# Row sums by ScalarE's queue in attention, an own tile for attention's output copy, DFT tables loaded in layer 0's last chunk, and z as the fourth chunk

## The chip, the core and the metric

The kernel runs on one core of a Trainium2 chip. The metric is the device time of one execution in microseconds (us); the time of a kernel is the median of its runs. The engines are named as in the profile: PE (TensorE matmuls) with PEld (its weight loads), DVE (VectorE), ACT (ScalarE), POOL (GpSimd) and SP (SyncE). SP only issues DMAs here; "SPq", "ACTq" and "POOLq" are DMA issues and waits in an engine's instruction queue.

## What is computed

A trunk of two layers over 2048 tokens of 1024 channels, in float32. Cut to what matters:

```python
# layer 0: norm, one projection, short gated convolution beside a Fourier mixer, output projection
a_x, a_b, a_c, a_z, b_u, b_z = split(rms_norm(x) @ w_in)          # 6 x 512 columns
y_a = a_b * conv3(a_c * a_x) * silu(a_z)
y_b = fft2(u by groups of 128 channels, axes=(tokens, channels)).real * silu(b_z)
x = x + concat([y_a, y_b]) @ w_out
# layer 1: norm, q/k/v/z projection, rotary, 8 query heads over 2 kv heads, softmax over all 2048 keys
o = softmax(q k^T / sqrt(128)) v
x = x + (o * silu(z)) @ w_out
out = rms_norm(x)
```

## The kernel before, in words

Every matrix is split into two fp32r parts, a high part (a cast, by ACT) and a low part (source minus high part, by DVE or POOL; `split`, lines 40 to 44), and every product is three matmuls (`mm3`, lines 56 to 60). The split of a large tile is therefore one ACT and one DVE (or POOL) instruction at lines 42 and 44. In the input projection of layer 0 a product of two 2 x 2 block matrices is done with seven block products instead of eight (`product`, lines 387 to 419): the operand blocks and their sums are called 11, s2, s3, s1, 12, 22, s4, and PE takes them in that order. After each block product a hook may run (`follow`), which is how other work is placed in the program beside a chunk.

**Layer 0's input projection** (`layer0_in`) goes through eleven chunks, i = 0 to 10. A conv chunk computes 128 channels of the convolution branch and ends in taps on ACT and DVE (lines 602 to 606) and products on POOL (lines 626 and 638); a simple chunk is u (copied out) or z (SiLU, line 659). Chunks 0 to 4 work on tokens 0 to 1023: the conv chunks 1, 2, 3, 4 and then z. Chunks 5 to 10 work on tokens 1024 to 2047: u, four conv chunks, z. The operands of the second half are made meanwhile by `operands` (lines 227 to 252), called four times through `prepare(k)` from hooks: each call takes three places of a small ring of tiles ("ring_o"), loads x, normalises it on DVE (line 433), forms sums and differences on POOL (line 240) and saves seven blocks to DRAM. After chunk 4 `load_operand` brings them back and splits them (line 44 once per half block).

**The Fourier mixer** (`fourier`) takes four groups g. `fold(c, g)` loads u of a group and folds it by its symmetries on DVE and POOL (lines 717 to 740, tile "uo"); `fold_transposes` turns the result on PE (tile "fqt"); then four products with DFT tables (tiles "fme" and "fm", PSUM "pfz"), a second, short transform (`second`), and a product with silu(z) (`finish`). Folds 0 and 1 run in hooks of chunk 10. The tables are loaded by GpSimd's queue at the head of `fourier` (lines 766 to 774). Operands, folds, tables and rings all come from one pool of nine large tiles, tag "S"; a tile can be taken when the last reader of the one before is done.

**Attention** (`Attention`) has 32 groups of one block of 128 queries and one kv head, with four heads each. Its order is written out by hand in lists of steps (`SLOT`, `DRAIN`): one slot per head and group, S score matmuls, M/C/N maximum, E exponent with row sums, T transposes of the probabilities (PE), H and L their split (ACT line 1356, DVE line 1360), O the product with v. PE, DVE, ACT and SP keep this order. Once per group G adds up the row sums and takes the reciprocal (line 1382), D writes them to DRAM (line 1389, tile "l" to "ld"), B reads them back as a broadcast (line 1398, tile "lb") together with z (line 1401, tile "az") and multiplies both on POOL (line 1403). When the last O of a group is done, `finish` copies the PSUM tile on ACT into the broadcast's own tile "lb" (line 1408) and POOL multiplies again (line 1409). There is one PSUM tile for O.

**The end of attention.** `DRAIN` is the slot list of the last groups. In it `layer1_out_start` issues the loads of the first operands ("a_o") and weights ("ring_r" from "wo") of the output projection, and ten steps W split them, one at a time, with the low parts on POOL. After attention `layer1_out` splits the rest, and PE starts the output projection (PSUM "po").

Outside attention only PE's order is fixed by hand; DVE, ACT, POOL and SP are ordered when the program is built, by a simulated timeline and priorities.

Of the kernel before, what the change touches and what calls it, by code (L numbers as in the profile page):

```python
# [15 lines left out]
F32 = mybir.dt.float32  # L16
F32R = mybir.dt.float32r
AF = mybir.ActivationFunctionType
ALU = mybir.AluOpType
# [4 lines left out]
P = 128  # L24
S = 2048
# [14 lines left out]
def split(nc, src, hi, lo, hi_eng="act", lo_eng="dve"):  # L40

    first = nc.vector.tensor_copy(hi, src) if hi_eng == "dve" else nc.scalar.copy(hi, src)  # L42
    eng = nc.vector if lo_eng == "dve" else nc.gpsimd
    return first.ins, eng.tensor_tensor(lo, src, hi, op=ALU.subtract).ins  # L44
# [377 lines left out]
def layer0_in(c):  # L422
# [64 lines left out]
    def mean(tb):  # L487
        d = None
        if tb < 2:
            d = c.RD0[tb] = c.dram.tile([4, P], F32, name=f"rd_n0_{tb}", tag=f"rd_n0_{tb}")  # L490
        bc[tb] = rstd_pe(c, [accs[:, tb * TB:(tb + 1) * TB] if tb < 2 else acc1[0][:, tb - 2]], f"n0_{tb}", TB, d)

    def bcast(tb):
        RB[tb] = c.evp.tile([P, TB], F32, tag="ev", name=f"rb_n0_{tb}")[:]
        nc.scalar.copy(RB[tb], bc[tb]())
# [157 lines left out]
    def simple_chunk(pr, W, dst, silu, name, hooks={}):  # L653
# [9 lines left out]

        st.product(W, out, f"p{name}_", hooks)

    def next_weights(i):
        return st.all_weights(c.w0[(i + 2) % 6 if i < 5 else i - 4], f"w{i + 1}")

    def norm1(x, j, k):
        norm(x, RB[2 + j], k)  # L670
# [1 line left out]
    def prepare(k):  # L672
        return lambda: st.operands(k, [c.x_T[2], c.x_T[3]], norm1)

    hooks = {0: first_hooks,
             2: {"s2": lambda: mean(2), "s1": lambda: (bcast(2), mean(3)),
                 "22": lambda: (bcast(3), st.held.clear()), "s4": prepare(0)},
             3: {"s2": prepare(1), "s1": prepare(2), "22": prepare(3)}, 10: c.fourier_first}
    for i in range(11):
        pr, ch = divmod(i, 5) if i < 5 else (1, i - 6)  # L680
        W = W0
        if 0 < i < 10:
            W0 = next_weights(i)
        if 0 <= ch < 4:
            conv_chunk(pr, ch, W, hooks.get(i, {}))
        elif ch == 4:
            simple_chunk(pr, W, c.bz, True, f"z{pr}", hooks.get(i, {}))
        else:
            simple_chunk(pr, W, c.uT, False, "u1")
        if i == 0:  # L690
            all_k("s4", d2)
            st.A.pop("21")
            w1("21", "t4", "22")
            start.__exit__(None, None, None)
            W0 = W1[0]
            stats1()
        if i == 4:
            for j, op in enumerate(A_OPS):
                st.load_operand(op, c.aT[j], "1")
            c.alt = c.evp.tile([P, TB], F32, name="alt", tag="ev")  # L700
            c.dm = c.evp.tile([P, 2, 2, P], F32R, name="dm", tag="ev")
            h = TB // 2
            nc.gpsimd.memset(c.alt[:, 0:h:2], 1.0)
            nc.gpsimd.memset(c.alt[:, 1:h:2], -1.0)
            nc.gpsimd.memset(c.alt[:, h:TB], 0.0)
            nc.gpsimd.dma_start(c.dm[:], c.dmat)
        if i == 9:
            nc.sync.dma_start(c.yT[1, 0:4, :, TB - 1].rearrange("c p -> p c"), yedge[:])
# [43 lines left out]
        split(nc, pt[:], qt[:, 0, j], qt[:, 1, j])  # L752


def fourier(c):


# [5 lines left out]
    zs, qa, dcos, nyqs = mix[:, 0:TB], mix[:, TB:TB + h], mix[:, TB + h:TB + h + P], mix[:, D - 16:D]  # L763
    xss = st.etile("fxs")
    fb = c.big.tile([P, 2, S], F32, tag="S", name="fb0")
    even = c.big.tile([P, 2, 2, 2, 2, h], F32R, tag="S", name="fme")
    for j in range(2):
        nc.gpsimd.dma_start(even[:, j], c.feven[j])
    M = []
    for j in range(2):  # L770
        m = c.big.tile([P, 2, 4, TB], F32R, tag="S", name=f"fm{j}")
        for i in range(2):
            nc.gpsimd.dma_start(m[:, i], c.fmat[j, i])
        M.append(m)
    nc.sync.dma_start(dcos, c.dcos_d)
    QT = c.QT
    NY = [None] * 4
# [438 lines left out]
class Attention:  # L1216
# [167 lines left out]
    def D(self, k):  # L1384
        if k % NTT:
            return
        st = self.st[k // NTT]
        st.d = self.c.dram.tile([4, P], F32, name=f"ld{st.name}", tag=f"ld{st.name}")
        self.nc.sync.dma_start(st.d[:].rearrange("h t -> t h"), st.l[:])

    def B(self, k):

        if k % NTT != 8:
            return
        st = self.st[k // NTT]
        c, nc, nm, d = self.c, self.nc, st.name, st.d
        st.rb = self.zp.tile([P, TB], F32, tag="rb", name=f"lb{nm}")
        nc.sync.dma_start(st.rb[:], d[:].rearrange("h t -> (h t)").partition_broadcast(P))
        qt, kvh = st.g
        st.zt = self.zp.tile([P, TB], F32, tag="z", name=f"az{nm}")  # L1400
        nc.sync.dma_start(st.zt[:].rearrange("p (h t) -> p h t", h=4),
                          c.zT[kvh * 4:kvh * 4 + 4].rearrange("h p t -> p h t")[:, :, qt * P:(qt + 1) * P])
        nc.gpsimd.tensor_tensor(st.zt[:], st.zt[:], st.rb[:], op=ALU.mult)  # L1403

    def finish(self, st):
        c, nc = self.c, self.nc
        qt, kvh = st.g
        c.last_copy = nc.scalar.copy(st.rb[:], st.po[:]).ins  # L1408
        nc.gpsimd.tensor_tensor(st.zt[:], st.zt[:], st.rb[:], op=ALU.mult)  # L1409
        self.ended.append(lambda: nc.sync.dma_start(  # L1410
            c.oT[qt // 4, kvh * 4:kvh * 4 + 4].rearrange("h p t -> p h t")[:, :, (qt % 4) * P:(qt % 4 + 1) * P],
            st.zt[:].rearrange("p (h t) -> p h t", h=4)))


def layer1_out_start(c, lp):

    nc = c.tc.nc
    st = c.pairs
    st.renew()
    c.W11 = tuple(lp.tile([P, 4, TB // 2], F32R, tag="w0", name=f"wo1_0_11{n}") for n in "hl")  # L1420
    st.A["11"] = st.atile("a11_o0")
    src = [c.oT[0], c.oT[1]]
    for k in (slice(0, 2), slice(2, 4)):
        st.fetch(st.raw("11", k), src, "11", k)
    c.wo1_raw = st.raw_weights(c.wo1[0])
    st.A["12"] = st.atile("a12_o0")
    for k in (slice(0, 2), slice(2, 4)):
        st.fetch(st.raw("12", k), src, "12", k)

    def w11(sl):  # L1430
        split(nc, c.wo1_raw["11"][:, sl], c.W11[0][:, sl], c.W11[1][:, sl], lo_eng="pool")

    return ([lambda k=k: st.split("11", k, "pool") for k in range(4)] + [lambda j=j: w11(slice(j, j + 2)) for j in (0, 2)]
            + [lambda k=k: st.split("12", k, "pool") for k in range(4)])


def layer1_out(c, lp):
# [128 lines left out]
def trunk_kernel(ctx, tc, x_T, g0, w0, cw, wo0, g1, w1, qg, kg, wo1, gf, cosT, sinT, fmat, feven, dmat, dcos, out_T, scratch=None):  # L1566
# [41 lines left out]
    with ExitStack() as es_w:  # L1608
        with ExitStack() as es_ps:
            c.ps = es_ps.enter_context(tc.tile_pool(name="ps", bufs=8, space=PSUM))  # L1610
            c.big = ctx.enter_context(tc.tile_pool(name="big", bufs=9))
            c.evp = ctx.enter_context(tc.tile_pool(name="ev", bufs=2))
            c.wp = es_w.enter_context(tc.tile_pool(name="w", bufs=8, side="right", reuse_waits="tile"))
            with ExitStack() as es_e:
                c.ep = es_e.enter_context(tc.tile_pool(name="e", bufs=4, side="right", reuse_waits="tile"))
                c.pairs = Pairs(c)
                c.QT = [None] * 4

                def fold0():
                    c.rb01 = c.pairs.gtile("rb01")[:, 0:D]  # L1620
                    for tb in range(2):
                        bcast_d(c, c.RD0[tb], f"u_{tb}", tile=c.rb01[:, tb * TB:(tb + 1) * TB])
                    c.fold0 = fold(c, 0)

                def fold1():
                    c.fold1 = fold(c, 1)

                c.fourier_first = {"s2": fold0, "12": fold1, "22": lambda: fold_transposes(c, 0, c.fold0[0])}
                layer0_in(c)
                c.pairs.renew()  # L1630
                fourier(c)
                layer0_out(c)
                layer1_in(c)
        c.fp = es_w.enter_context(tc.tile_pool(name="zf", bufs=3, side="right", reuse_waits="tile"))
        load_kv(c)
        es_q = ctx.enter_context(ExitStack())
        qp = es_q.enter_context(tc.tile_pool(name="attq", bufs=2, reuse_waits="tile"))
        es_a = ctx.enter_context(ExitStack())
        pools = [es_a.enter_context(tc.tile_pool(name=n, bufs=b, space=PSUM, reuse_waits="tile"))
                 for n, b in (("pss", 4), ("pst", 3), ("pso", 1))]  # L1640
        fill = c.filler(pools[1])
        for _ in range(7):
            next(fill)
        att = Attention(c, qp, *pools, groups, fill, [6, 6, 6, 5, 2])
        for n in range(5):
            att.slot(n, att.FIRST)
            if n == 1:
                c.silu_z(att.exp.ins)
# [113 lines left out]
```

## Time and profile before

| | |
|---|---|
| median of 3 runs | 2339.57 us (2337.32 to 2339.77) |
| the profiled execution's own time | 2335.91 us |
| its span, first to last instruction | 2334.1 us |
| busy: PE / DVE / ACT / POOL | 2265.6 / 1531.9 / 1201.3 / 571.1 us |
| mean granted TensorE clock | 0.990 |
| moved by DMA | 413.99 MB, mean 177 GB/s |

A row of the timeline has the start, the duration, the engine, the line, the operation, "out<-in" by tile names, the shapes and a count of merged instructions; in brackets stands the idle time of the engine just before it and what ended that. A row of the list of waits has who waited for whom, the total, the number of times and the longest. A row of the stretches has each engine's busy time in that stretch, PE's granted clock, the mean busy share of the 16 DMA engines and their rate. The four groups of work stand in the span at about these places: layer 0's input projection up to 514 us, the Fourier mixer to 586, the output projection of layer 0 and the projections of layer 1 to 1200, attention to 2125, the output projection of layer 1 to the end.

### The profile page before, as it was taken

Reading aid. Unit: us, or ns where it says so; the run is one execution under the profiler, and the core shown is the slowest. Engines: PE = TensorE matmul, PEld = TensorE weight load, DVE = VectorE, ACT = ScalarE, POOL = GpSimd, SP = SyncE. Lnnn points to the kernel's source line nnn. Section 1 sums busy time; section 2 is a strip of 40 time slices with the busy share of each in tenths; the row PEclk is TensorE's granted clock in tenths of the full one; section 3 lists DMA queues with packets and bytes.
Section 4 is the critical chain, followed back from the end, with each engine's and each line's share of the span. In section 5 each row is a group of like instructions: output and inputs, shape, how many; then the busy total and the mean of one; then the engine's idle time right before and its main releaser. Section 6 shows DMA issues by size and latency. Waiting matters only on the chain. (4 is left out here: it accounts for less than half of the span.)

```text
span 2334.1 us, 34356 instructions
## 1 busy us (share of the span) xinstructions
PE 2265.6 (97%) x12450; PEld 1917.2 (82%) x12450; DVE 1531.9 (66%) x2469; ACT 1201.3 (51%) x2638; POOL 571.1 (24%) x418
## 2 busy tenths in 40 slices
PE   9989899988999999999999999999999999997998
PEld 7877688877888899889987888888888888886887
DVE  7967867679642445425548888788788788775235
ACT  5442432224332345424547777777777777775212
POOL 2566535444232132103201100010001000003212
PEclk9999999999999999999999999999999999998999
DMA  4244742247756534533566767676666676668553
GB/s 164 86 149 155 253 138 73 63 171 268 266 187 201 145 119 134 163 102 127 171 235 185 205 203 202 196 200 204 193 200 197 193 195 198 201 187 269 180 189 127
DMA packets 260281, 413.99 MB, mean 177 GB/s; under 512 B 37136, under 2 KB 157072, under 8 KB 258320
## 3 DMA queue, kind: packets, MB, share of 16 engines
q1 hardware_dynamic: 257840, 404.17, 55.0%
q0 software_dynamic: 1008, 6.55, 0.8%
q8 instruction: 99, 1.62, 0.3%
q10 hardware_dynamic: 1264, 1.07, 0.1%
q14 instruction: 70, 0.57, 0.1%
HBM read 190.92 MB, written 86.59 MB: 119 GB/s over the span
## 5 line engine op out<-in xcount | busy, mean ns | idle before, releaser
L1314 DVE TENSOR_REDUCE mx<-s 128x1 f32<-128x512 f32 x512 | 351.0, 687 | 172.6 <-PE s L60 170.9
L1333 ACT ACTIVATE praw<-s,nb,qs 128x512 f32<-128x512 f32 x512 | 401.3, 800 | 18.2 <-DVE nb L1323 12.1
L1356 ACT CAST pr<-t 128x512 fp32r<-128x512 f32 x512 | 290.8, 600 | 181.7 <-PE t L1344 181.7
L1360 DVE TENSOR_TENSOR pr<-t,pr 128x512 fp32r<-128x512 f32 x512 | 329.3, 680 | 13.2 <-ACT pr L1356 11.4
L1344 PEld LDWEIGHTS t<-ident_r,P 128*128 128x128 f32 x2048 | 202.0, 140 | 36.9 <-DVE pr L1360 1.1
L58 PE MATMUL o<-pr,kv 128*128 128x512 f32 x512 | 212.2, 414 | 2.5 <-ACT pr L1356 2.1
L58 PE MATMUL s<-kv,aq 128*128 128x512 f32 x512 | 211.0, 412 | 2.4 <-DMA aq<-qT 1.2
L1344 PE MATMUL t<-ident_r,P 128*128 128x128 f32 x2048 | 203.8, 243 | 0.9 <-DVE pr L1360 0.9
L60 PE MATMUL o<-pr,kv 128*128 128x512 f32 x512 | 202.5, 395 | 0.0
L59 PE MATMUL o<-pr,kv 128*128 128x512 f32 x512 | 202.2, 395 | 0.2 <-DVE pr L1360 0.2
L60 PE MATMUL s<-kv,aq 128*128 128x512 f32 x512 | 201.9, 394 | 0.0
L59 PE MATMUL s<-kv,aq 128*128 128x512 f32 x512 | 200.8, 392 | 0.0
L1403 POOL TENSOR_TENSOR az<-az,lb 128x512 f32<-128x512 f32 x32 | 41.4, 1295 | 477.6 <-DMA az<-zT 454.8
L958 POOL TENSOR_TENSOR acc<-acc,sq 128x512 f32<-128x512 f32 x48 | 69.0, 1438 | 228.4 <-ACT sq L956 210.5
L60 PEld LDWEIGHTS o<-pr,kv 128*128 128x128 f32 x512 | 96.2, 188 | 23.2
L60 PEld LDWEIGHTS s<-kv,aq 128*128 128x128 f32 x512 | 96.1, 188 | 22.5
L58 PEld LDWEIGHTS s<-kv,aq 128*128 128x128 f32 x512 | 95.8, 187 | 21.3 <-ACT praw L1333 3.2
L1333 ACT ACTIVATION_READ_ACCUMULATOR praw<-s,nb,qs 128x1 f32 x512 | 112.7, 220 | 0.0
L58 PEld LDWEIGHTS o<-pr,kv 128*128 128x128 f32 x512 | 96.0, 187 | 19.7 <-ACT pr L1356 2.5
L59 PEld LDWEIGHTS o<-pr,kv 128*128 128x128 f32 x512 | 96.5, 188 | 17.7 <-DVE pr L1360 0.5
L59 PEld LDWEIGHTS s<-kv,aq 128*128 128x128 f32 x512 | 96.3, 188 | 17.2
L1409 POOL TENSOR_TENSOR az<-az,lb 128x512 f32<-128x512 f32 x32 | 42.0, 1311 | 253.0 <-ACT lb L1408 250.1
(644 smaller groups left out, 5836.8 us busy)
## 6 DMA issues: line engine op xcount, KB each, us to landing
P<-praw SPq DMA_DIRECT2D x256, 512.0 KB
ring_r<-w SPq DMA_DIRECT2D x80, 512.0 KB
ring_o<-x_T SPq DMA_DIRECT2D x32, 512.0 KB
ring_r<-wo SPq DMA_DIRECT2D x32, 512.0 KB
qT<-ring_o SPq DMA_DIRECT2D x64, 256.0 KB
aq<-qT SPq DMA_DIRECT2D x31, 512.0 KB
x1T<-po_t SPq DMA_DIRECT2D x16, 512.0 KB
a_x<-x1T SPq DMA_DIRECT2D x16, 512.0 KB
```

What stands on the lines that cost most here:

```text
L58: nc.tensor.matmul(ps, lh, rh, start=first, stop=False, skip_group_check=shared)
L59: nc.tensor.matmul(ps, lh, rl, start=False, stop=False, skip_group_check=shared)
L60: nc.tensor.matmul(ps, ll, rh, start=False, stop=last, skip_group_check=shared)
L958: nc.gpsimd.tensor_tensor(a, a, sq, op=ALU.add)
L1314: self.nc.vector.tensor_reduce(st.mx[h][:, b:b + 1], st.banks[h, b][:], op=ALU.max, axis=AX.X)
L1333: self.exp = nc.scalar.activation(raw[:, b % 2], st.banks.pop((h, b))[:], AF.Exp, bias=st.nb[h][:], scale=self.c.qs[:, st.g[0], st.g[1], h ...
L1344: self.nc.tensor.transpose(pt[:, h * P:(h + 1) * P].bitcast(F32R), st.Ps[h // 2][:, h % 2, kt // 8, (kt % 8) * P:(kt % 8 + 1) * P], self.c ...
L1356: self.nc.scalar.copy(pr[:, 0], pt[:])
L1360: self.nc.vector.tensor_tensor(pr[:, 1], pt[:], pr[:, 0], op=ALU.subtract)
L1403: nc.gpsimd.tensor_tensor(st.zt[:], st.zt[:], st.rb[:], op=ALU.mult)
L1409: nc.gpsimd.tensor_tensor(st.zt[:], st.zt[:], st.rb[:], op=ALU.mult)
```

## The change

1. **Order of the chunks.** A list gives the order: 1, 2, 3, 5, 4 for the first half of the tokens, so that z comes fourth and the last conv chunk fifth; the second half is as before. The four calls of `prepare` move into the z chunk, behind its products 11, s3, 12 and s4.
2. **DFT tables.** Their loads, still by GpSimd's queue, move into hooks of chunk 10: the even table behind product s3, the two odd ones behind s1 and 12. `fold(c, 1)` moves out of that chunk to a place just ahead of `fourier`.
3. **Row sums.** D writes the 128 x 4 reciprocals as 128 rows of four, by ScalarE's queue, instead of transposed as four rows of 128 by SyncE's queue. B reads the broadcast in that order, and POOL's first product takes it through a strided view. The load of z moves from B to D, two slots earlier.
4. **Copy of attention's PSUM.** `finish` copies into a tile of its own ("oc", one buffer) instead of into "lb".
5. **Splits at the end of attention.** Of the ten W steps the low parts are made by DVE instead of POOL, and the weights' two steps come behind the first two steps of operand 11 instead of behind all four.

```diff
+    chunks = (1, 2, 3, 5, 4, 0, 1, 2, 3, 4, 5)
...
     hooks = {0: first_hooks,
-             2: {"s2": lambda: mean(2), "s1": lambda: (bcast(2), mean(3)),
-                 "22": lambda: (bcast(3), st.held.clear()), "s4": prepare(0)},
-             3: {"s2": prepare(1), "s1": prepare(2), "22": prepare(3)}, 10: c.fourier_first}
+             2: {"s2": lambda: mean(2), "s1": lambda: (bcast(2), mean(3)), "22": lambda: (bcast(3), st.held.clear())},
+             3: {"11": prepare(0), "s3": prepare(1), "12": prepare(2), "s4": prepare(3)}, 10: c.fourier_first}
...
+def load_even(c):
+    c.even = c.big.tile([P, 2, 2, 2, 2, TB // 2], F32R, tag="S", name="fme")
+    for j in range(2):
+        c.tc.nc.gpsimd.dma_start(c.even[:, j], c.feven[j])
+
+def load_odd(c, j):
+    m = c.big.tile([P, 2, 4, TB], F32R, tag="S", name=f"fm{j}")
+    for i in range(2):
+        c.tc.nc.gpsimd.dma_start(m[:, i], c.fmat[j, i])
+    c.M.append(m)
...
     def D(self, k):
...
-        st.d = self.c.dram.tile([4, P], F32, name=f"ld{st.name}", tag=f"ld{st.name}")
-        self.nc.sync.dma_start(st.d[:].rearrange("h t -> t h"), st.l[:])
+        st.d = c.dram.tile([P, 4], F32, name=f"ld{nm}", tag=f"ld{nm}")
+        nc.scalar.dma_start(st.d[:], st.l[:])
+        st.zt = self.zp.tile([P, TB], F32, tag="z", name=f"az{nm}")
+        nc.sync.dma_start(st.zt[:].rearrange("p (h t) -> p h t", h=4),
+                          c.zT[kvh * 4:kvh * 4 + 4].rearrange("h p t -> p h t")[:, :, qt * P:(qt + 1) * P])
...
     def B(self, k):
...
-        nc.sync.dma_start(st.rb[:], d[:].rearrange("h t -> (h t)").partition_broadcast(P))
-        nc.gpsimd.tensor_tensor(st.zt[:], st.zt[:], st.rb[:], op=ALU.mult)
+        nc.sync.dma_start(rb[:], st.d[:].rearrange("t h -> (t h)").partition_broadcast(P))
+        zt = st.zt[:].rearrange("p (h t) -> p h t", h=4)
+        nc.gpsimd.tensor_tensor(zt, zt, rb[:].rearrange("p (t h) -> p h t", h=4), op=ALU.mult)
...
     def finish(self, st):
...
-        c.last_copy = nc.scalar.copy(st.rb[:], st.po[:]).ins
-        nc.gpsimd.tensor_tensor(st.zt[:], st.zt[:], st.rb[:], op=ALU.mult)
+        o = self.zp.tile([P, TB], F32, tag="o", name=f"oc{st.name}", bufs=1)
+        nc.scalar.copy(o[:], st.po[:])
+        nc.gpsimd.tensor_tensor(st.zt[:], st.zt[:], o[:], op=ALU.mult)
...
-    return ([lambda k=k: st.split("11", k, "pool") for k in range(4)] + [lambda j=j: w11(slice(j, j + 2)) for j in (0, 2)]
-            + [lambda k=k: st.split("12", k, "pool") for k in range(4)])
+    return ([lambda k=k: st.split("11", k) for k in range(2)] + [lambda j=j: w11(slice(j, j + 2)) for j in (0, 2)]
+            + [lambda op=op, k=k: st.split(op, k) for op, ks in (("11", (2, 3)), ("12", range(4))) for k in ks])
...
-                c.fourier_first = {"s2": fold0, "12": fold1, "22": lambda: fold_transposes(c, 0, c.fold0[0])}
+                c.M = []
+                c.fourier_first = {"s2": fold0, "s3": lambda: load_even(c), "s1": lambda: load_odd(c, 0), "12": lambda: load_odd(c, 1),
+                                   "22": lambda: fold_transposes(c, 0, c.fold0[0])}
                 layer0_in(c)
                 c.pairs.renew()
+                c.fold1 = fold(c, 1)
                 fourier(c)
```

More of the change, by code (lines that the diff above doesn't have):

```diff
@@ L664, in simple_chunk @@
         st.product(W, out, f"p{name}_", hooks)
+    chunks = (1, 2, 3, 5, 4, 0, 1, 2, 3, 4, 5)
     def next_weights(i):
-        return st.all_weights(c.w0[(i + 2) % 6 if i < 5 else i - 4], f"w{i + 1}")
+        return st.all_weights(c.w0[chunks[i + 1]], f"w{i + 1}")
     def norm1(x, j, k):
@@ L675, in layer0_in @@
     hooks = {0: first_hooks,
-             2: {"s2": lambda: mean(2), "s1": lambda: (bcast(2), mean(3)),
-                 "22": lambda: (bcast(3), st.held.clear()), "s4": prepare(0)},
-             3: {"s2": prepare(1), "s1": prepare(2), "22": prepare(3)}, 10: c.fourier_first}
-    for i in range(11):
-        pr, ch = divmod(i, 5) if i < 5 else (1, i - 6)
+             2: {"s2": lambda: mean(2), "s1": lambda: (bcast(2), mean(3)), "22": lambda: (bcast(3), st.held.clear())},
+             3: {"11": prepare(0), "s3": prepare(1), "12": prepare(2), "s4": prepare(3)}, 10: c.fourier_first}
+    for i, n in enumerate(chunks):
+        pr, ch = i // 5, n - 1
         W = W0
@@ L683, in layer0_in @@
             W0 = next_weights(i)
[L684 to L687, printed above, removed]
+        if n in (1, 2, 3, 4):
+            conv_chunk(min(pr, 1), ch, W, hooks.get(i, {}))
+        elif n == 5:
+            simple_chunk(min(pr, 1), W, c.bz, True, f"z{pr}", hooks.get(i, {}))
         else:
-            simple_chunk(pr, W, c.uT, False, "u1")
+            simple_chunk(1, W, c.uT, False, "u1")
         if i == 0:
@@ L765, in fourier @@
     fb = c.big.tile([P, 2, S], F32, tag="S", name="fb0")
[L766 to L774, printed above, removed]
+    even, M = c.even, c.M
     nc.sync.dma_start(dcos, c.dcos_d)
@@ L1387, in D @@
         st = self.st[k // NTT]
-        st.d = self.c.dram.tile([4, P], F32, name=f"ld{st.name}", tag=f"ld{st.name}")
-        self.nc.sync.dma_start(st.d[:].rearrange("h t -> t h"), st.l[:])
+        c, nc, nm = self.c, self.nc, st.name
+        st.d = c.dram.tile([P, 4], F32, name=f"ld{nm}", tag=f"ld{nm}")
+        nc.scalar.dma_start(st.d[:], st.l[:])
+        qt, kvh = st.g
+        st.zt = self.zp.tile([P, TB], F32, tag="z", name=f"az{nm}")
+        nc.sync.dma_start(st.zt[:].rearrange("p (h t) -> p h t", h=4),
+                          c.zT[kvh * 4:kvh * 4 + 4].rearrange("h p t -> p h t")[:, :, qt * P:(qt + 1) * P])
     def B(self, k):
@@ L1395, in B @@
         st = self.st[k // NTT]
[L1396 to L1403, printed above, removed]
+        nc, nm = self.nc, st.name
+        rb = self.zp.tile([P, TB], F32, tag="rb", name=f"lb{nm}")
+        nc.sync.dma_start(rb[:], st.d[:].rearrange("t h -> (t h)").partition_broadcast(P))
+        zt = st.zt[:].rearrange("p (h t) -> p h t", h=4)
+        nc.gpsimd.tensor_tensor(zt, zt, rb[:].rearrange("p (t h) -> p h t", h=4), op=ALU.mult)
     def finish(self, st):
@@ L1430, in w11 @@
     def w11(sl):
-        split(nc, c.wo1_raw["11"][:, sl], c.W11[0][:, sl], c.W11[1][:, sl], lo_eng="pool")
-    return ([lambda k=k: st.split("11", k, "pool") for k in range(4)] + [lambda j=j: w11(slice(j, j + 2)) for j in (0, 2)]
-            + [lambda k=k: st.split("12", k, "pool") for k in range(4)])
+        split(nc, c.wo1_raw["11"][:, sl], c.W11[0][:, sl], c.W11[1][:, sl])
+    return ([lambda k=k: st.split("11", k) for k in range(2)] + [lambda j=j: w11(slice(j, j + 2)) for j in (0, 2)]
+            + [lambda op=op, k=k: st.split(op, k) for op, ks in (("11", (2, 3)), ("12", range(4))) for k in ks])
 def layer1_out(c, lp):
@@ L1623, in fold0 @@
                     c.fold0 = fold(c, 0)
-                def fold1():
-                    c.fold1 = fold(c, 1)
-                c.fourier_first = {"s2": fold0, "12": fold1, "22": lambda: fold_transposes(c, 0, c.fold0[0])}
+                c.M = []
+                c.fourier_first = {"s2": fold0, "s3": lambda: load_even(c), "s1": lambda: load_odd(c, 0), "12": lambda: load_odd(c, 1),
+                                   "22": lambda: fold_transposes(c, 0, c.fold0[0])}
                 layer0_in(c)
                 c.pairs.renew()
+                c.fold1 = fold(c, 1)
                 fourier(c)
```

## The prediction

> **What bounds the kernel now.** I read the page first, then PE's waits, then the busy time by stretch, then the timeline at the places where PE waits.
>
> ```profile
> span 2334.1 us, 34356 instructions
> PE 2265.6 (97%) x12450; PEld 1917.2 (82%) x12450; DVE 1531.9 (66%) x2469; ACT 1201.3 (51%) x2638; POOL 571.1 (24%) x418
> ```
>
> PE is the bound, and its number of matmuls does not change. So only the 68 us in which it stands idle, and the time after an idle stretch in which its clock is halved, can be won. The list of PE's waits says for whom it waits:
>
> ```profile
> PE po L58 <- ACT lb L1408: 9.9, 1, 9.9
> PE pa_s L58 <- DVE pa_u L395: 6.0, 2, 5.7
> ...
> PE pfz L59 <- DMA fm<-fmat: 4.7, 2, 2.7
> PE pz L60 <- DVE w_21l L44: 4.7, 1, 4.7
> PE pfz L58 <- DMA fm<-fmat: 3.3, 1, 3.3
> PE pfz L58 <- DMA fme<-feven: 2.5, 2, 1.4
> ...
> PE o L58 <- ACT pr L1356: 2.1, 1, 2.1
> ...
> PE pa_s L58 <- DVE pa_w L395: 1.8, 1, 1.8
> PE pz_s L58 <- DVE pz_w L395: 1.7, 1, 1.7
> ...
> PE po L60 <- POOL wo_11l L44: 1.3, 1, 1.3
> ...
> PE pz_s L60 <- DVE w_t1l L44: 1.1, 1, 1.1
> ```
>
> These belong to three places, which the change touches one each: the z chunk of layer 0 (w_21l, w_t1l, pz_w) with the chunk before it (pa_w), the start of the Fourier mixer (fm, fme), and the end of attention (lb, pr, wo_11l). The 5.7 us at pa_u lie in chunk 2, where nothing is changed. The busy time by stretch (PE, PEld, DVE, ACT, POOL, then PE's granted clock, the DMA share and GB/s) prices the clock; the second row is undisturbed:
>
> ```profile
> 230.00:281.00 51.00, 43.52 (x175) 34.44 (x174) 40.48 (x36) 18.11 (x23) 31.00 (x23) 0.93 0.75 237
> 350.00:400.00 50.00, 50.00 (x220) 41.02 (x219) 35.12 (x36) 14.98 (x19) 23.12 (x12) 1.00 0.22 70
> 473.00:508.00 35.00, 34.50 (x158) 28.26 (x156) 29.00 (x36) 8.67 (x12) 20.84 (x16) 1.00 0.28 106
> 508.00:541.00 33.00, 22.51 (x97) 17.80 (x98) 18.16 (x39) 8.69 (x17) 11.27 (x14) 0.84 0.94 353
> 541.00:597.00 56.00, 51.77 (x278) 43.55 (x277) 55.91 (x76) 25.31 (x39) 23.87 (x16) 1.00 0.77 271
> 1250.00:2100.00 850.00, 850.00 (x4869) 707.47 (x4868) 682.85 (x1289) 635.81 (x1492) 82.42 (x75) 1.00 0.68 197
> 2104.00:2118.00 14.00, 13.63 (x92) 11.43 (x91) 8.07 (x15) 6.94 (x13) 2.49 (x2) 1.00 0.25 32
> 2121.00:2145.00 24.00, 10.85 (x32) 7.95 (x33) 12.22 (x9) 12.91 (x19) 17.02 (x12) 0.72 1.06 377
> ```
>
> The clock that is not granted is length times one minus the clock: 0.07 x 51 = 3.6 us in the z chunk, 0.16 x 33 = 5.3 us at the Fourier start, 0.28 x 24 = 6.7 us at the end of attention. From 1250 to 2100 PE is busy for all of 850 us at full clock: steady attention has nothing to give.
>
> **The change part by part.**
>
> *Copy of PSUM, splits, row sums: the end of attention.* One row of SP's waits there, then rows of SP's, ACT's, POOL's and DVE's timelines:
>
> ```profile
> SPq L1389 <- DVE l L1382: 4.0, 1, 4.0
> 2105.92 12.31 SPq L273 DMA_DIRECT2D ring_r<-wo  x4
> ...
> 2123.66 1.41 SPq L1398 DMA_DIRECT2D lb<-ld  x1
> 2119.67 1.14 ACT L42 CAST a_o<-a_o 128x512 fp32r<-128x512 f32 x2 [3.26 <-DMA a_o<-oT]
> ...
> 2136.41 0.58 ACT L1408 COPY lb<-o 128x512 f32<-128x512 f32 x1
> 2132.89 1.26 POOL L1403 TENSOR_TENSOR az<-az,lb 128x512 f32<-128x512 f32 x1 [4.07 <-DMA az<-zT]
> 2110.35 2.69 DVE L1360 TENSOR_TENSOR pr<-t,pr 128x512 fp32r<-128x512 f32 x4 [1.55 <-ACT pr L1356]
> 2114.55 2.69 DVE L1360 TENSOR_TENSOR pr<-t,pr 128x512 fp32r<-128x512 f32 x4 [1.50 <-issue]
> 2135.19 2.57 DVE L44 TENSOR_TENSOR a_o<-a_o 128x1024 fp32r<-128x1024 f32 x2 [4.16 <-ACT a_o L42]
> ```
>
> The broadcast of the last group is issued at 2123.66, behind the weights; POOL's first product can only run at 2132.89; the copy overwrites that product's input and so comes at 2136.41; and PE's first output product waits 9.9 us for the PSUM tile. With a tile of its own the copy needs only the last O. The whole wait goes. The 2.1 us at pr come from ACT standing for 3.26 us before a split whose operand has not landed: the loads behind the row sums crawl (32 GB/s from 2104 to 2118, SP held 12.31 us in four issues). In the new program z's load and a_o's no longer stand behind SP's wait of 4.0 us for the reciprocal, and 128 writes of 16 bytes take the place of 512 of 4. The slow stretch is about 12 us now; for 128 writes I bound it by 0 and 12 and take a quarter, 3 us, by their number. Either way most of a_o is under way before it. So 2.1 goes, and 1.3 at wo_11l with it, since DVE makes the low part. Sum: 9.9 + 2.1 + 1.3 + 6.7 of clock = 20.0 us.
>
> What is late next: the ten splits are new work for DVE. Two slots of 4.20 us (the two starts above) hold 2.69 us of DVE work and get three splits each, of 0.69:
>
> ```profile
> 596.78 0.69 DVE L44 TENSOR_TENSOR a_y<-ring_r,a_y 128x512 fp32r<-128x512 f32 x1
> ```
>
> That is 4.76 in 4.20: 1.1 us over for two slots. And operand 21, whose split ends at 2135.19 + 2.57 before, is wanted two block products (5.5 us each: 24 matmuls at 220 in 50 us) after attention's end, so it may be the next that is late; I allow 0.9 us. So **18 us**, between 8 (the copy early, all else late) and 20.
>
> *Steady attention.* The row sums' issue on ACT is new there; before it has ACT's price only in other places, and in each group ACT waits before the copy:
>
> ```profile
> L1580 ACTq DMA_DIRECT2D cws<-cw x1: 453/453/453, 2.1 to 2.1; - x1
> 2001.94 0.59 ACT L1408 COPY lb<-o 128x512 f32<-128x512 f32 x1 [1.36 <-issue]
> ```
>
> D stands in the same slot as that copy and ahead of it, so 0.45 us fall into an idle time of 1.36: cost **0**, behind it casts and exponents wait otherwise, and PE for them. POOL's strided product has a cover as well, 82 us busy of 850. What is cheaper here buys nothing, as PE is full.
>
> *DFT tables.* The row of their first issue, their sizes with the median time to landing, PE's last product of chunk 10, and the busy time (PE, PEld, DVE, POOL) of the four folds:
>
> ```profile
> 508.11 1.14 POOL L768 DMA_DIRECT2D fme<-feven  x2
> fm<-fmat POOLq DMA_DIRECT2D x4, 1024.0 KB, 17.9
> fme<-feven POOLq DMA_DIRECT2D x2, 1024.0 KB, 8.4
> 513.74 0.40 PE L60 MATMUL pz_s<-as,w_22l 128*128 128x512 f32 x1
> 473.00:600.00 127.00, 8.27 (x64) 7.71 (x64) 32.72 (x52) 31.20 (x28) 0.96 0.69 249
> ```
>
> Issued at 508, six loads of 1 MB can't be there at 514. Behind s3, s1 and 12 they start four, three and two products (22, 16 and 11 us) and the transposes earlier; at 353 GB/s six megabytes take 18 us, and the DMA share of 473 to 508 is 0.28. So they are there when PE comes. The waits of 4.7 + 3.3 + 2.5 and 5.3 of clock go: 15.8 us at most. But from 541 to 597 DVE is busy for 55.91 of 56 us: it is the second bound, and PE can only come forward as far as DVE does. DVE's idle time from 508 to 541 is 33 - 18.16 = 14.8 us, and fold 1, which now comes behind the tables, needs a quarter of the 32.72 us of the folds: 8.2 us. That leaves 6.6; some of the fold still fits ahead of 508, where DVE loses that load. I take **8 us**, between 3 and 15.8.
>
> *Order of the chunks.* All four waits there, 1.8 + 1.1 + 4.7 + 1.7 = 9.3 us and 3.6 of clock, 12.9 in sum, are for DVE, and in DVE's queue, ahead of what PE wants, stand the 16 norms of `prepare`, which wait 18.8 us for x:
>
> ```profile
> L433 DVE SCALAR_TENSOR_TENSOR ring_o<-ring_o,g0s,rb_n 128x512 f32<-128x512 f32 x16 | 19.0, 1230 | 18.8 <-DMA ring_o<-x_T 18.8
> ```
>
> The z chunk has no taps on DVE and no products on POOL, so `prepare` finds both freer there. But the work is only moved: the taps now meet the splits of the seven operands in chunk 4, and each `prepare` comes one product, 5.5 us, later, in a ring whose places still come free only when the call before has saved. A third of it, **4 us**; bounds -8 (a wait like 4.7 with its clock of 3.6 more) and 12.9.
>
> Sum: 18 + 0 + 8 + 4 = 30 us. Against the profiled execution's own 2335.9 that is 2305.9; the median of the runs stands 3.7 higher, so **2309.6 us**.
>
> **The Trainium skill against the trace.** "DMA: Bandwidth & Descriptors", section "Issuing engines are not separate DMA queues", says that DMAs of ScalarE, SyncE and GpSimd run interleaved on the same 16 engines, and that a second issuing engine only saves issue time. It speaks against moving the row sums to ACT. The row 2104:2118 (share 0.25 at 32 GB/s) fits engines that are held rather than full, whoever issued. By that rule the way through ACT helps nothing; no row of before has ACT issuing in attention, so that stays open. The sum above counts nothing for the engine.
>
> **The rivals.**
> *The slow loads stay* (the mechanism beside which the skill's rule stands): the 128 writes hold the loads as long as 512 did, so 2.1 and 1.3 stay and operand 21 comes no earlier, some 2 us; the gain at the end is 13 instead of 18: 2314.6. For: no row tells what in the write is slow. Against: a_o goes ahead of it.
> *DVE takes it back*: Fourier gains only 3, and the chunk order costs 5 as DVE is fuller in chunks 4 and 5: 18 + 3 - 5 = 16: 2323.6. For: 55.91 of 56.
> *All of it*: 20.0 + 15.8 + 12.9 = 48.7: 2290.9. Against: the same row.
> *ACT's queue is held* (slower): if the issue on ACT blocks as SP's does in the row of 2105.92, 12.31 / 4 = 3.1 us, it outlasts the 1.36 by 1.7 us in each of 31 groups, and PE with it: 53 us lost, 23 after the 30 gained: 2362.6. It decides from 1.36 + 30 / 31 = 2.3 us per issue on. Against: that was a queue with megabytes ahead of it, ACT's own queue has nothing else.
> *The copy is not early*: if the built order still puts the copy behind the casts of the next stage, which are not bound to the hand-written order, the end gains 4: 2323.6 again.
>
> **How the numbers follow.** Forecast 0.56, slow loads 0.10, DVE takes it back 0.17, copy not early 0.04, all of it 0.07, ACT held 0.06. Two runs of this kernel can be told apart from about 0.2% on, 4.7 us. Each case but ACT held is faster by more; a bad mixture of the lower ends (8 + 3 - 8) is within it: faster 0.91, same 0.04, slower 0.05. The range goes from 2294, towards all of it, to 2328, beyond DVE takes it back; outside lie ACT held and half of all of it and of the tails.
>
> **What would show it.** No wait of PE on line 1408's copy and clock 1.00 from 2121 on; the copy right behind the last O; a_o landed before its splits want it. No wait of pfz on fm or fme, but more waits on DVE's fqt or fmix between 514 and 590. Fewer than 9.3 us of waits in chunks 3 to 5. Steady attention still at 850 of 850. The prediction is wrong in kind if PE waits for pr in every group, and in its sums if the Fourier part gives 15 or the chunk order loses time.

## The result, and the profile after

| | median of the runs | profiled execution | its span |
|---|---|---|---|
| before | 2338.45 us (2335.07 to 2339.77, 4 runs) | 2335.91 us | 2334.1 us |
| after | 2317.49 us (2315.12 to 2319.89, 4 runs) | 2315.25 us | 2313.5 us |

The ratio is 0.9913, with an interval from 0.9895 to 0.9931: the change gains about 21 us where 30 were forecast. The time is inside the range.

First PE's waits in the changed kernel, in the same columns as before (total, times, longest):

```profile
...
PE pfz L60 <- DVE fqt L44: 4.5, 2, 2.4
...
PE pt L752 <- DVE uo L737: 3.2, 1, 3.2
...
PE pa_s L58 <- DVE pa_w L395: 2.9, 1, 2.9
PE py L58 <- DVE fz L44: 2.9, 1, 2.9
PE pz_s L58 <- DVE pz_w L395: 2.2, 1, 2.2
...
PE pa L58 <- ACT w_t4h L42: 1.5, 1, 1.5
...
PE po L58 <- ACT oc L1417: 0.5, 1, 0.5
```

The 9.9 us for the copy are now 0.5, and the rows for pr, wo_11l, fm and fme are gone. But the Fourier part has three rows that it did not have or had shorter (fqt, uo, fz), all for DVE, and the chunks have w_t4h in place of w_21l. The stretches of the changed kernel say the same with the clock (the columns are PE, PEld, DVE, ACT, POOL, granted clock, DMA share, GB/s):

```profile
230.00:281.00 51.00, 45.79 (x184) 36.34 (x183) 32.85 (x31) 21.07 (x25) 27.66 (x17) 0.93 0.85 284
473.00:508.00 35.00, 35.00 (x163) 28.97 (x162) 22.84 (x34) 10.41 (x16) 13.89 (x15) 1.00 0.78 284
508.00:541.00 33.00, 28.83 (x146) 24.75 (x145) 31.04 (x51) 9.92 (x18) 18.81 (x16) 0.90 0.49 179
541.00:597.00 56.00, 48.65 (x237) 40.93 (x236) 50.32 (x67) 24.62 (x36) 20.20 (x15) 0.91 0.81 282
1250.00:2100.00 850.00, 850.00 (x4869) 707.50 (x4868) 682.85 (x1288) 634.14 (x1490) 89.97 (x74) 1.00 0.56 198
2104.00:2118.00 14.00, 13.90 (x90) 11.63 (x90) 9.80 (x16) 9.62 (x20) 1.29 (x1) 1.00 1.05 358
2121.00:2145.00 24.00, 23.49 (x103) 19.27 (x103) 21.96 (x22) 15.68 (x20) 16.98 (x3) 1.00 0.85 296
```

At the end of attention PE is busy for 23.49 of 24 us at clock 1.00, where it had 10.85 at 0.72. The tables do load between 473 and 508 (284 GB/s instead of 106). Yet from 541 to 597 the clock fell from 1.00 to 0.91: 0.09 x 56 = 5.0 us not granted there, more than the 0.06 x 33 = 2.0 us won just before. Both are upper bounds of what it cost, since a low clock costs nothing while PE is idle.

Where the 20.6 us of span came from is read from PE's timeline at three places. First the kernel before, then the one after: the first product with the DFT tables, the first product of the output projection behind the mixer, the first score of attention.

```profile
515.54 0.36 PE L58 MATMUL pfz<-fme,fqt 128*128 128x256 f32 x1 [1.40 <-DMA fme<-feven]
585.68 0.48 PE L58 MATMUL po<-a_y,wo_11h 128*128 128x512 f32 x1
1206.32 0.47 PE L58 MATMUL s<-kv,aq 128*128 128x512 f32 x1 [1.21 <-DMA aq<-qT]
```

```profile
513.24 0.28 PE L58 MATMUL pfz<-fme,fqt 128*128 128x256 f32 x1
583.07 0.48 PE L58 MATMUL po<-a_y,wo_11h 128*128 128x512 f32 x1
1203.36 0.47 PE L58 MATMUL s<-kv,aq 128*128 128x512 f32 x1 [1.93 <-DMA aq<-qT]
```

Up to attention 3.0 us are won, 2.3 of them by the first of the three rows and 2.6 by the second. From the first score to the end of the span it was 2334.1 - 1206.32 = 1127.8 us and is 1110.1: 17.7 us. The chunks gave nothing: the second half of layer 0 (the first product of chunk 6) starts at 319.22 before and at 319.20 after.

### The profile page after: what moved, and what is told of

The parts are those of the page before. It is cut to its first block, busy times and chain, and to the rows that moved or that the text cites. A ratio compares the mean times of both kernels' runs of the same rounds, so it can differ in the third digit from the quotient of the medians.

```text
span 2313.5 us, 34304 instructions
## 1 busy us (share of the span) xinstructions
PE 2265.7 (98%) x12450; PEld 1920.2 (83%) x12450; DVE 1530.3 (66%) x2479; ACT 1198.4 (52%) x2638; POOL 574.8 (25%) x408
## 5 line engine op out<-in xcount | busy, mean ns | idle before, releaser
L1411 POOL TENSOR_TENSOR az<-az,lb 128x512 f32<-128x512 f32 x32 | 61.8, 1930 | 442.6 <-DMA lb<-ld 407.3
L1418 POOL TENSOR_TENSOR az<-az,oc 128x512 f32<-128x512 f32 x32 | 42.2, 1318 | 286.2 <-ACT oc L1417 286.1
L58 PEld LDWEIGHTS o<-pr,kv 128*128 128x128 f32 x512 | 96.0, 187 | 16.9 <-ACT oc L1417 0.2
```

Of the source, the lines that this page charges most:

```text
L58: nc.tensor.matmul(ps, lh, rh, start=first, stop=False, skip_group_check=shared)
L1411: nc.gpsimd.tensor_tensor(zt, zt, rb[:].rearrange("p (t h) -> p h t", h=4), op=ALU.mult)
L1418: nc.gpsimd.tensor_tensor(st.zt[:], st.zt[:], o[:], op=ALU.mult)
```

## The experiments

Theory: the end of attention gives what was forecast; the tables gave less because fold 1 came too late; the order of the chunks only moves waits. The main rival: the parts are worth what was predicted and something else takes 9 us back. Twelve runs were made, in three groups of four, each group on one chip. The kernel before took 2331 us beside two of the groups and 2338 beside the third, as in the result, so ratios and gains are against the kernel before on the same chip.

**The parts, one at a time.** Each is the kernel before with one numbered part of the change.

`e1_order`, part 1 alone:

```diff
+    chunks = (1, 2, 3, 5, 4, 0, 1, 2, 3, 4, 5)
...
+             3: {"11": prepare(0), "s3": prepare(1), "12": prepare(2), "s4": prepare(3)}, 10: c.fourier_first}
```

> The kernel before with the order of the chunks alone (z fourth, the four prepare calls in its hooks). Theory: the waits of PE on DVE in chunks 3 to 5 are only moved, since the same norms, taps and operand splits must pass through DVE before 320 us; no change, within 3 us of the kernel before, and PE reaches the first conv chunk of the second half (line 58, chunk 6) at 318 to 321 us in the span as in the kernel before (319.2). Rival: the order is worth the 4 us of the prediction and something else in the whole change eats it; then this kernel is 4 to 8 us faster, and chunk 6 starts at 311 to 315 us.

`e2_tables`, part 2 alone:

```diff
+                c.fourier_first = {"s2": fold0, "s3": lambda: load_even(c), "s1": lambda: load_odd(c, 0), "12": lambda: load_odd(c, 1),
...
+                c.fold1 = fold(c, 1)
                 fourier(c)
```

> The kernel before with the DFT tables in chunk 10 and fold 1 moved out of it, nothing else. Theory: the waits on the tables (10.5 us) go, and fold 1, now loaded only after the tables and folded beside fold 2, makes PE wait for its transposes and DVE be late for the rest; gain 1 to 4 us, with waits on uo, fqt and fz of 10 us or more between 514 and 585 us. Rival: the small gain of the whole change at this place is an accident of how that build was ordered together with the chunk order; then this alone gains the predicted 8 us or more.

`e3_rows`, part 3 alone, the copy still into "lb":

```diff
+        nc.scalar.dma_start(st.d[:], st.l[:])
...
+        rb = st.rb = self.zp.tile([P, TB], F32, tag="rb", name=f"lb{nm}")
```

> The kernel before with the row sums alone (128 rows of four by ScalarE's queue, z loaded at D, strided first product), the copy still into lb. Theory: the loads at the end of attention are no longer held, so the waits of PE on pr (2.1 us) and on wo_11l (1.3 us) go and the broadcast lands earlier; the copy still waits for POOL's product, and PE for the copy, but less long: gain 4 to 10 us. Steady attention stays at 850 of 850 us. Rival: the copy is what counts and the row sums give nothing; then it is within 3 us of the kernel before and the 12 us issue of the weights stays.

`e4_copy`, part 4 alone:

```diff
+        o = self.zp.tile([P, TB], F32, tag="o", name=f"oc{st.name}", bufs=1)
+        nc.scalar.copy(o[:], st.po[:])
```

> The kernel before with the copy of attention's PSUM in its own tile alone. Theory: the wait of 9.9 us and most of the 6.7 us of lost clock behind it go: gain 12 to 17 us, while the waits on pr and wo_11l stay. Rival: the next operand is as late as the copy was, because the loads behind the row sums still crawl; then PE waits for a_o or a weight instead and the gain is 3 to 8 us.

`e5_splits`, part 5 alone:

```diff
-    return ([lambda k=k: st.split("11", k, "pool") for k in range(4)] + [lambda j=j: w11(slice(j, j + 2)) for j in (0, 2)]
+    return ([lambda k=k: st.split("11", k) for k in range(2)] + [lambda j=j: w11(slice(j, j + 2)) for j in (0, 2)]
```

> The kernel before with the ten splits moved from POOL to VectorE alone. Theory (the three fixes stand one behind the other; the copy still waits for POOL's product, which waits for z's load): only the wait of 1.3 to 1.9 us for wo_11l goes, 0 to 3 us faster than before. Rival (the splits are the 7 us that copy and row sums together leave of the gain, by themselves): 5 to 9 us faster.

| | median, us | before, same chip | ratio (interval) | gain, us |
|---|---|---|---|---|
| e1_order | 2332.09 | 2331.36 | 1.0000 (0.9988 to 1.0012) | 0 |
| e2_tables | 2328.03 | 2331.36 | 0.9984 (0.9975 to 0.9994) | 3.7 |
| e3_rows | 2326.04 | 2331.36 | 0.9977 (0.9968 to 0.9986) | 5.4 |
| e4_copy | 2325.33 | 2331.36 | 0.9980 (0.9971 to 0.9990) | 4.7 |
| e5_splits | 2328.34 | 2331.07 | 0.9990 (0.9980 to 0.9999) | 2.3 |

The gain is one minus the ratio, times the time before. The order is worth nothing and the tables 3.7 us, as the theory had it; with the tables alone PE waits 3.8, 3.6 and 3.2 us for uo, fqt and fz. Rows and splits lie within what was expected of them (4 to 10 and 0 to 3). The copy was a miss: 12 to 17 were expected and 4.7 came, so the rival named there holds. PE's waits at the output projection in the run with the copy alone, and the rows of SP and of POOL that lead there:

```profile
PE po L59 <- POOL a_o L44: 3.7, 2, 3.1
...
PE po L60 <- POOL wo_11l L44: 1.9, 1, 1.9
```

```profile
2111.15 10.34 SPq L273 DMA_DIRECT2D ring_r<-wo  x4
...
2135.66 2.12 POOL L1403 TENSOR_TENSOR az<-az,lb 128x512 f32<-128x512 f32 x1 [4.84 <-DMA az<-zT]
2137.74 7.94 POOL L44 TENSOR_TENSOR a_o<-a_o 128x512 fp32r<-128x512 f32 x4
```

The wait for the PSUM tile is gone, but the loads still crawl (SP held for 10.34 us), and POOL makes the next operand's low parts behind its product for z: PE comes to them one block product later and waits again. Three causes stand one behind the other, and the one removed uncovers the next.

**Two causes together.** `e10_copy_rows` has parts 3 and 4, without the splits; `e0_after` is the whole change again, on the same chip.

> The kernel before with the own tile for the copy and the new row sums together, the splits of the next stage's operands still on POOL. Alone the copy gained 6 us and the row sums 5.3. Theory (three things stand one behind the other: the copy, the loads, the splits on POOL): with the first two gone PE waits for POOL's low parts, 2 us for wo_11l and 2 to 4 for the next operand with a halved clock behind them: 7 to 10 us faster than before. Rival (the splits cost nothing, as POOL has room once its product is early): 13 to 16 us faster.

> The changed kernel itself, beside the parts. In the runs of the single parts the kernel before took 2331 us where the result has 2338, and their traces miss a wait of PE for wo_22l (2.5 us and the clock behind it) that the traces of before and after both show. Theory: that wait belongs to neither kernel, so the change still gains 18 to 21 us here. Rival: a part of the 20 us of the result is such a wait and not the change: 12 to 16 us.

The whole change took 2316.47 us against 2337.56, ratio 0.9912 (0.9895 to 0.9929), as in the result. Copy and rows together took 2328.73, ratio 0.9959 (0.9943 to 0.9974): 9.6 us won, as the theory expected, but perhaps not all by its causes: a wait for wo_22l late in the output projection, for which neither part is meant, is 2.5 us in the trace of the kernel before and 1.0 here. What PE waits for then is the third cause:

```profile
PE po L59 <- POOL a_o L44: 2.4, 1, 2.4
...
PE po L60 <- POOL wo_11l L44: 1.9, 1, 1.9
```

and the stretch behind attention, with copy and rows:

```profile
2118.00:2145.00 27.00, 22.69 (x90) 17.72 (x90) 22.84 (x16) 20.60 (x28) 23.17 (x12) 0.87 1.05 374
```

The same stretch in the run with the whole change:

```profile
2118.00:2145.00 27.00, 26.49 (x116) 21.38 (x115) 23.37 (x27) 19.25 (x24) 18.06 (x3) 1.00 0.88 304
```

The two waits (4.3 us) and 0.13 x 27 = 3.5 us of clock make 7.8 us. By the ratios the whole change gains 20.6 us here; without the 3.7 of the tables that is 16.9, which is 7.3 more than copy and rows. Alone the splits gained 2.3, in combination about 7.

The traces allow a comparison without the kernel before. From the first score of attention to the end of the span it is 1121 us in the runs with the order alone and with the tables alone, which leave this part as it was; 1115 with the copy alone, 1115 with the rows alone, and 1115 with both; 1118.5 with the splits alone; and 1107 in `e6b_fold1` and `e8_fold1_order_back` below, which have all three parts. As far as these chips compare (copy and rows together ran where the kernel before takes 2338 us, the others where it takes 2331), copy and rows win 6 us whether one of them is there or both, and the splits some 8 more behind them: 14 us. On the chip of the result the same stretch goes from 1128 to 1110; what the kernel before has more there is seen in its waits for pr (2.1 us) and wo_22l (2.5 us and the clock behind it). The run of the whole change, made on a chip of that kind, confirms the 20.6 us there, but does not decide between its two expectations for the other chips.

**Writes or issuer.** `e11_rows4_act` is the changed kernel with 512 writes of 4 bytes, but still from ACT's queue and with z's load ahead; `e9_rows_sp` is the changed kernel with its 128 writes of 16 bytes issued by SP.

```diff
-        st.d = c.dram.tile([P, 4], F32, name=f"ld{nm}", tag=f"ld{nm}")
-        nc.scalar.dma_start(st.d[:], st.l[:])
+        st.d = c.dram.tile([4, P], F32, name=f"ld{nm}", tag=f"ld{nm}")
+        nc.scalar.dma_start(st.d[:].rearrange("h t -> t h"), st.l[:])
```

> The changed kernel with the row sums written by ScalarE's queue but turned as before, 512 writes of 4 bytes, and read as before. Theory (the writes' number holds the loads, whoever issues them): loads issued behind the last write crawl again for about 11 us; with z's and a_o's loads ahead of it half of that is covered: 2 to 6 us slower than the changed kernel. Rival (the engine that issues is what counts): within 1 us of the changed kernel.

```diff
-        nc.scalar.dma_start(st.d[:], st.l[:])
+        nc.sync.dma_start(st.d[:], st.l[:])
```

> The changed kernel with SyncE issuing the row sums' 128 writes instead of ScalarE. Theory (the number and size of the writes is what holds the loads; SyncE only adds its wait for the reciprocal, 4.0 us in the trace of before, ahead of z's and a_o's loads): 0 to 4 us slower than the changed kernel. Rival (the queue that issues counts as much as the writes): 8 to 14 us slower, as with the 512 writes from ScalarE.

The 512 writes from ACT took 2330.46 us, ratio 0.9966 (0.9953 to 0.9979): 14 us slower than the changed kernel on the same chip by the medians and 12.6 by the ratios, more than twice the 2 to 6 expected of the theory. By the traces 12.6 us lie behind the first score and 2.9 ahead of it, where the writes do not act. Here are SP's issues around the last row sums of that run, then ACT's rows behind them, then what PE waits for:

```profile
2108.51 3.42 SPq L273 DMA_DIRECT2D ring_r<-wo  x4
...
2117.34 8.96 SPq L218 DMA_DIRECT2D a_o<-oT  x4
```

```profile
2132.29 1.04 ACT L42 CAST a_o<-a_o 128x1024 fp32r<-128x1024 f32 x1 [5.02 <-DMA a_o<-oT]
...
2134.60 0.58 ACT L1416 COPY oc<-o 128x512 f32<-128x512 f32 x1
```

```profile
PE po L58 <- ACT oc L1416: 6.0, 1, 6.0
```

The weights ahead of the writes are issued in 3.42 us, but a_o's loads behind them hold SP for 8.96. The copy has its own tile and needs nothing but the last O; but on ACT it stands behind casts of those loads, waits with them for 5.02 us, and PE for it. So the own tile makes the copy early only if the loads ahead of it in ACT's order have landed. Some 7 of the 12.6 us lie behind the first output product, the rest in attention, 1.7 of it a low clock at its start.

With 128 writes from SP the run took 2316.76 us where before took 2331.07, ratio 0.9939 (0.9925 to 0.9954). That is a gain of 14 us. The whole change was not run on that chip, so this ratio can't be set directly against 0.9912, and whether the run is within 0 to 4 us of the changed kernel is not measured; the traces can be compared. From the first score to the end of the span this run has 2315.3 - 1205.86 = 1109.4 us, the two traces of the changed kernel 1110.1 and 1108.6. SP's issues behind its write:

```profile
2105.56 0.34 SPq L1396 DMA_DIRECT2D ld<-l  x1
...
2107.48 4.20 SPq L273 DMA_DIRECT2D ring_r<-wo  x4
```

Four weight loads in 4.20 us, against 12.31 before, though SP issues the writes in both: it is the writes, not who issues them. The Trainium skill ("DMA: Bandwidth & Descriptors", "Issuing engines are not separate DMA queues") says that a second issuing engine saves no more than issue time; this agrees.

**Fold 1 earlier.** `e6_fold1` is the changed kernel with fold 1 called in the hook of 12, ahead of the second odd table, in place of behind the last chunk. `e6b_fold1` is the same kernel on another chip, beside `e8_fold1_order_back`, which also has the chunk order and prepares of the kernel before.

```diff
-"12": lambda: load_odd(c, 1),
+"12": lambda: (fold1(), load_odd(c, 1)),
...
-                c.fold1 = fold(c, 1)
```

> The changed kernel with fold 1 called in the hook of 12 again, ahead of the second odd table, in place of behind the last chunk. Theory (fold 1's late load, at 505.41 behind z's stores in SP's queue, and its running beside fold 2 ate the tables' gain): its load is issued before 500, PE's wait of 3.2 us for uo and part of the 4.5 for fqt go, 3 to 6 us faster than the changed kernel. Rival (VectorE is full in this stretch whatever the order): within 2 us of the changed kernel, other waits in place of these.

> The changed kernel with fold 1 in the hook of 12, once more, beside the variant with the old chunk order. Theory: 24 to 28 us faster than before, as in its first run (26.6).

> Fold 1 in the hook of 12, and the chunk order, the prepares and their hooks as in the kernel before; copy, row sums, splits and tables as changed. Theory (the order is worth nothing, as in its run alone): within 2 us of the run with the new order. Rival (with the rest of the change the order pays what was predicted for it): 3 to 5 us slower than that.

The first run took 2310.94 us, ratio 0.9877 (0.9861 to 0.9893): faster than the changed kernel on its chip by 5.5 us by the medians, inside the theory's 3 to 6, and by 8.2 by the ratios, above it. SP's wait at z's first store in the changed kernel, the places of u's loads for the folds, and its two folds on POOL:

```profile
SPq L662 <- ACT pz_w L659: 19.6, 1, 19.6
```

```profile
505.41 0.38 SPq L720 DMA_DIRECT2D uo<-uT  x1
507.28 0.38 SPq L720 DMA_DIRECT2D uo<-uT  x1
```

```profile
512.29 3.44 POOL L724 TENSOR_TENSOR uo<-uo 128x1023 f32<-128x1023 f32 x1 [13.51 <-DVE uo L721]
...
518.52 2.82 POOL L724 TENSOR_TENSOR uo<-uo 128x1023 f32<-128x1023 f32 x1
```

Fold 1's load leaves at 505.41, behind z's stores in SP's queue, and fold 2's two microseconds later. POOL, idle for 13.51 us until then, and DVE work on both at once, where PE already wants the products. With the call in the hook both first loads are issued between 482.96 and 492.66, the second after a wait for a product of PE, and the start of the output projection and of attention come forward. First the two loads, SP's wait at the second, then the two starts:

```profile
482.96 9.70 SPq L720 DMA_DIRECT2D uo<-uT  x2
```

```profile
SPq L720 <- PE pz_s L60: 8.9, 1, 8.9
```

```profile
575.21 0.48 PE L58 MATMUL po<-a_y,wo_11h 128*128 128x512 f32 x1
1195.72 0.47 PE L58 MATMUL s<-kv,aq 128*128 128x512 f32 x1 [1.09 <-DMA aq<-qT]
```

That is 7.9 and 7.6 us ahead of the changed kernel's, although chunk 6 started 2.7 us later in this run. It is the fastest execution of its four (2305.77 us, the others 2310.48 and more), so this is more than is typical. From the first DFT product to the output projection it takes 59.3 us, and 64.1 in the second run of the same kernel, against 69.8 and 70.9 in the two traces of the changed kernel. The wait of 8.9 us, which fits a wait for a place among the tiles, suggests that the load's turn in the pool counts as well as its turn in SP's queue. The hook moves both, and which of them is worth how much was not tried.

With the order of before as well it took 2302.53 us, ratio 0.9879 (0.9864 to 0.9894); its neighbour with the new order 2308.09, ratio 0.9899 (0.9882 to 0.9915). It is the fastest kernel here, 28.5 us ahead of before. The new order gained 23.5 us by its ratio, just below the 24 to 28 expected, and for the old order theory and rival were both wrong: it was better by 5.6 us. The two intervals overlap, but no run of the one is as slow as the fastest of the other. PE's waits in chunks 3 to 5, first with the new order, then with the old one:

```profile
PE pa L58 <- ACT w_t4h L42: 4.6, 1, 4.6
PE pa_s L58 <- DVE pa_w L395: 1.9, 1, 1.9
PE pu_s L60 <- DVE w_t1l L44: 1.5, 1, 1.5
```

```profile
PE pz L60 <- DVE w_21l L44: 4.6, 1, 4.6
PE pz_s L58 <- DVE pz_w L395: 1.5, 1, 1.5
PE pa_s L58 <- DVE pa_w L395: 1.2, 1, 1.2
```

The long wait for w_21l is replaced by one for w_t4h of the chunk that now comes last: 1.5 to 4.6 us in each of seven traces with the new order, while w_21l costs 3.0 to 4.7 in each of seven with the old one. From the first product of chunk 0 to that of chunk 6 the new order takes 265.9 us on average (263.9 to 267.7), the old one 263.8 (262.4 to 264.9). So it gains nothing and probably loses some 2 us. Of the 6.3 us by which the spans of the two neighbours differ, 4.6 lie in this stretch: it is 267.7 us in the one, the longest of all, and 263.1 in the other. Whether that is the order or chance is not settled: the order alone measured 0 with an interval of 2.8 us to either side.

## Why the prediction was right, and where it was not

*End of attention: right in sum, not in its shares.* 18 us were forecast, the two traces give 17.7, and on the other chips it is 14. The clock is 1.00 behind attention, the copy stands right behind the last O, and the waits for pr and wo_11l are gone. The changed kernel's timeline has ACT's issue of the last row sums, the start of the output projection and that copy:

```profile
2104.03 0.33 ACTq L1396 DMA_DIRECT2D ld<-l  x1
...
2120.21 0.39 PE L58 MATMUL po<-a_o,wo_11h 128*128 128x512 f32 x1
...
2120.93 0.59 ACT L1417 COPY oc<-o 128x512 f32<-128x512 f32 x1
```

The step "with a tile of its own the copy needs only the last O. The whole wait goes" did not hold by itself: alone it gave 4.7. The splits were given the 1.3 us of wo_11l; they are worth about 7 where copy and loads are early. And "the slow loads stay" was priced at 5 us lost; with 512 writes left in place 12.6 were lost from the first score on, since the late loads also hold the copy in ACT's order. The guess of a quarter of the hold for a quarter of the writes was not tried by itself; a_o was there in time.

That the sum fits is in part luck, since its term for the clock was too large. The kernel before, from the stretch where the clock falls on:

```profile
2129.00:2137.00 8.00, 0.00 (x0) 0.00 (x0) 3.72 (x4) 2.59 (x4) 1.26 (x1) 0.51 1.06 382
2137.00:2145.00 8.00, 7.96 (x23) 6.34 (x24) 4.21 (x3) 4.03 (x7) 7.94 (x5) 0.63 1.05 387
```

In the first row 0.49 x 8 = 3.9 us of clock are not granted, but PE has nothing to run (0.00 busy), so they cost nothing beyond the wait of 9.9 that is counted already. Only the second row's 0.37 x 8 = 3.0 us could be won, not 6.7. What made up for it are the two costs of the next paragraph and some 2 us at wo_22l, which the sum does not have: the wait went from 2.5 to 1.9 us, and the clock behind it (0.58 from 2289 to 2293, so 1.7 us) stayed at 1.00.

*The two costs allowed there did not appear.* PE has no wait for pr in the drain, against 1.1 us allowed, and none for operand 21, against 0.9.

*Steady attention: right.* 850 of 850 us; ACT's issue of the row sums costs 0.33 us a group in place of the 0.45 taken.

*DFT tables: right kind, wrong size.* 8 us were forecast; 3.7 were measured alone and 3.0 up to attention in the whole. The failed step is "some of the fold still fits ahead of 508": none of fold 1 did, as its load left at 505.41 and its first operation on DVE began at 510.93. The step weighed DVE's time, of which there was enough, and did not follow the load of the step it moved through SP's queue. The fold came back as waits for fqt, uo and fz (4.5 us, of which 2.4 were there before, 3.2 and 2.9), and up to 5.0 us of clock. With the load early 6 to 12 us more come off the mixer.

*Order of the chunks: wrong.* 4 us were forecast, 0 measured. The failed step is the third taken of the 12.9 us because `prepare` "finds both freer there": the waits are 8.3 us in sum where they were 9.3, mostly on other tiles. The prediction had itself said that the work is only moved, and that part held.

*Of the rivals*, "DVE takes it back" came closest outside the end of attention: 3 us for the Fourier part, as it said, and an order that does not pay; its 5 us of loss there are more than the order showed by itself. ACT's queue is not held: 0.33 us against the 2.3 from which that rival would decide. The copy is early.

## What to carry to other kernels

When a step is moved, follow its loads through the queue that issues them: a fold placed "just behind" a stage waits for that stage's stores if they share a queue. When PE stands at the end of a stage, look for what is second and third in line there, since a fix for the first alone may give less than half of the whole, and test the fixes together. Count a low clock only where the engine has work. Write small results so that each write is as long as it can be, whoever issues it, before anything large is loaded behind them.

## What the runs showed of the hardware

The 512 writes of 4 bytes cost other transfers DMA time. The share of the 16 engines that the large transfers' queue took, with 512 writes and with 128, both issued by ACT through another queue (packets, MB, share):

```profile
q1 hardware_dynamic: 240944, 404.11, 60.2%
```

```profile
q1 hardware_dynamic: 240944, 404.11, 51.0%
```

The same packets and bytes took 0.602 x 2328.8 = 1402 us of all 16 engines in place of 0.510 x 2313.3 = 1180, which is 6.9 us more for each of 32 groups. From 1250 to 2100 us that cost PE almost nothing (848.84 us busy of 850); from the first score to the end it cost 12.6 us. How the writes hold the others was not tried.

POOL's product through the strided view takes 1.56 us in steady attention instead of 1.30. The last one, beside DVE's splits, took 13.33 us, and cost nothing that shows: PE waits for nothing behind it. It is 14.7 to 15.3 us long in four more runs that have parts 3 to 5 and 1.67 in the one with SP's writes, where it starts ahead of the splits and one of them takes 2.06 us instead of 0.69. The Trainium skill ("GPSIMD Engine Reference", "Specifications") says that GpSimd's way to SBUF is shared with VectorE and contended when VectorE's instruction has two SBUF inputs, as the splits have; the row fits it:

```profile
2122.66 13.33 POOL L1411 TENSOR_TENSOR az<-az,lb 128x512 f32<-128x512 f32 x1 [15.85 <-ACT a_o L42]
```

The chips differ, or what goes with them: where the kernel before takes 2338 us, PE waits 0.9 to 2.5 us for wo_22l in the last projection in all of the six traces; where it takes 2331, in none of eight. Where that comes from is open.
